# Modulation and gate vectors as TensorE strips instead of elementwise sums, with the recurrence's products regrouped

## The chip, the core and the metric

The kernel runs on one core of a Trainium2 chip. The metric is the device time of one execution in microseconds (us). Three executions of the kernel before took 2051.42, 2052.46 and 2072.93 us, median 2052.46. One further execution was profiled; all rows below come from it.

The engines are named as the profile names them: PE is TensorE, which multiplies, PEld is its loading of the stationary operand, DVE is VectorE, ACT is ScalarE, POOL is GpSimd, SP is SyncE, whose queue issues most transfers (DMAs). TensorE's results go to PSUM, in banks of 128 x 512 fp32.

## What is computed

A two-layer trunk over 256 latent and 256 context tokens of width 2048. A conditioning vector is turned into a shift, a scale and a gate for each layer, once for latent (`sc`) and once for context tokens (`scc`):

```python
sc = jax.nn.silu(c)
scc = jax.nn.silu(c_ctx)
for l in range(DEPTH):                       # 2 layers
    shift_l, scale_l, gate_l = split(sc @ mod_w[l] + mod_b[l])     # mod_w[l]: 2048 x 6144
    shift_c, scale_c, gate_c = split(scc @ mod_w[l] + mod_b[l])
    hl = xl * (1.0 + scale_l) + shift_l
    hc = xc * (1.0 + scale_c) + shift_c
    # layer 0: one input projection -> [pooling mixer | bidirectional RWKV-7] -> gate -> output projection
    # layer 1: one input projection -> attention -> gate -> output projection
    xl = layer_norm(ALPHA * xl + gate_l * yl, ln_g[l], ln_b[l])
    if not last: xc = layer_norm(ALPHA * xc + gate_c * yc, ln_g[l], ln_b[l])
```

The RWKV recurrence (16 heads, both directions) is computed in 8 chunks of 64 tokens: inside a chunk by Gram matrices and a triangular inverse, from chunk to chunk through a 64 x 64 state per head.

## The kernel before

Large weights come as fp32, are split into two fp32r halves (`whi` by ACT, `wlo` by POOL or DVE, lines 192 and 74), and every product is made of three fp32r matmuls (`mm3`): rows `acc<-hh,whi`, `acc<-hl,whi`, `acc<-hh,wlo`, each 128 x 128 by 128 x 512. These are the filling. The small products of the recurrence are fp32; the trace shows each fp32 product as two rows, and it names operands moving one first or last, so `cz<-AR,S` and `cx<-S,AR` are both products of a state `S` with `AR`.

What stands where on TensorE is written by a planner: TensorE's order is the order of recording (`manual_schedule`), the other engines are ordered by a scheduler. Each process is a Python generator that records some products and yields a number of microseconds; `merge` runs the process of the highest priority that is ready by an estimated time `self.t`, to which `mm` (line 86 issues every product) adds a cost. `share` scales that cost. The processes are

- `rwkv`, with one pass of 8 heads-pairs `p`: `prep(p+1)` and its `gram`s run while `chain(p)` runs; then `by_token`, `inverse`, `join`;
- `chain`: 8 steps `c`. A step makes `cx` = state times `AR`, adds `NV` on DVE to get `R`, then `cz` = `X` times `R`, copied to `U` by DVE and ACT, then `cs` = `BKT` times `U` for the next state, then the output `cy`: for each of four quadrants (2 directions x 2 heads) a product `GR` x `U` over all 128 rows and a product `S` x `AR` over 64 rows, in turn;
- `gram`: per direction, groups of four products of 64 rows x 128 columns, one head after the other, into the two banks `tr`;
- `fill0`: the input projection of layer 0 (to about 1290 us), then the output projection (`out0`) and layer 1;
- `gemvs0` and `gemvs1`: gates and layer 1's modulation. For each of 32 pieces of 256 columns, 8 loads of 256 KB (`gw`); DVE multiplies by the latent vector and adds (line 782); for the context vector ACT multiplies in place (line 778) and POOL adds (line 785). At a piece's end `gemv_end` sums over the partitions on TensorE (with `ones`, or four transposes and a DVE reduction). 24 pieces run beside the recurrence, the last 8 (only the latent vector, DVE alone) beside layer 1's projections;
- layer 0's modulation (`mod_units`, `mod_cols`) is already made on TensorE in the first 150 us: the vectors stand as 32 columns (`sc`), four 32-column strips of the array take four row blocks of the weights side by side, and a product with `comb` folds the strips.

`prep` and `tr` are PSUM tags of two banks, `cx` and `cz` of one each.

Of the kernel before, what the change touches and what calls it, by code (L numbers as in the profile page):

```python
# [14 lines left out]
KT = D // 128  # L15
# [21 lines left out]
class Kern:  # L37
# [50 lines left out]
    def tp(self, out, x, ident):  # L88
        self.t += 0.058
        self.nc.tensor.transpose(out, x, ident)  # L90
# [41 lines left out]
    def setup(self):  # L132
        nc, io, cp = self.nc, self.io, self.cp
        self.par = cp.tile([128, NPAR], F32, name="par")
        nc.sync.dma_start(self.par, io["par"])
        self.cv = cv = cp.tile([128, 32], F32, name="cv")
        nc.scalar.activation(cv, self.par[:, COL["cvec"]:COL["cvec"] + 32], AF.Silu)
        self.modc = [cp.tile([128, KT, 2, 2], F32, name=f"modc{i}") for i in range(2)]

    def setup2(self):  # L140
# [15 lines left out]
        self.ones = cp.tile([128, 1], F32, name="ones")  # L156
        nc.vector.memset(self.ones, 1.0)
# [39 lines left out]
    def mod_units(self, w, n, tag, done):  # L197


        nc = self.nc  # L200
        ps = []

        def f(q):
            def g(t):
                if q == 0:
                    ps.append(self.pt(tag, (128, n)))
                for j in range(4):
                    self.mm(ps[0][32 * j:32 * j + 32, :], self.sc[:, 4 * q + j, :], t[:, j * n:(j + 1) * n], start=(q == 0), stop=(q == KT // 4 - 1), share=0.25)
                yield 0.0
                if q == KT // 4 - 1:  # L210
# [5 lines left out]
        return [(w[:, q * 4 * n:(q + 1) * 4 * n], f(q), True) for q in range(KT // 4)]  # L216

    def mod_cols(self, layer, which, k0, n, tag, then=None):

        def done(row):  # L220
            yield 2.0
            nk = n // 128
            pc = self.pt("prep", (128, nk, 2))
            for j in range(nk):
                self.mm(pc[:, j, :], row[:, j * 128:(j + 1) * 128], self.comb)
            b = COL["modb"] + layer * 48 + which * KT + k0
            self.nc.vector.scalar_tensor_tensor(out=self.modc[layer][:, k0:k0 + nk, which, :], in0=pc, scalar=float(which),
                                                in1=self.par[:, b:b + nk].unsqueeze(2).to_broadcast([128, nk, 2]), op0=ALU.add, op1=ALU.add)
            if then:
                yield from then()  # L230
        return self.mod_units(self.io["modA"][which * 8 + k0 // 2], n, tag, done)
# [4 lines left out]
    def begin(self):  # L236
# [5 lines left out]
        with self.tc.tile_pool(name="beg", bufs=3) as bp:  # L242
            wp = self.wp
            self.wset(bp, 1024, 8, 6)

            self.sc = bp.tile([128, KT, 32], F32, name="sc", bufs=1)
            nc.gpsimd.memset(self.sc, 0.0)
# [1140 lines left out]
```

## Time and profile before

| | us |
|---|---|
| median of three executions | 2052.46 |
| the profiled execution | 2059.26 |
| its span, first to last instruction | 2057.4 |
| PE busy | 1845.3 (90%) |
| DVE busy | 1397.4 (68%) |
| POOL busy | 984.7 (48%) |
| ACT busy | 891.0 (43%) |
| mean granted TensorE clock | 0.942 of 2.4 GHz |

From 0 to 150 us the first modulation and projections run, from 150 to about 1250 the recurrence with the input projection as filling, to about 1500 layer 0's output projection, to 1660 the keys and values of layer 1, then attention and the last projection. In a timeline row the first number is the start, the second the length; rows of one line that follow each other are merged (xcount). Products are pipelined, so a row's length is longer than its distance to the next row, and the distance is what a product costs.

### The profile page before, as it was taken

Reading aid. Unit: us, or ns where it says so; the run is one execution under the profiler, and the core shown is the slowest. Engines: PE = TensorE matmul, PEld = TensorE weight load, DVE = VectorE, ACT = ScalarE, POOL = GpSimd, SP = SyncE. Lnnn points to the kernel's source line nnn. Section 1 sums busy time; section 2 is a strip of 40 time slices with the busy share of each in tenths; the row PEclk is TensorE's granted clock in tenths of the full one; section 3 lists DMA queues with packets and bytes.
Section 4 is the critical chain, followed back from the end, with each engine's and each line's share of the span. In section 5 each row is a group of like instructions: output and inputs, shape, how many; then the busy total and the mean of one; then the engine's idle time right before and its main releaser. Section 6 shows DMA issues by size and latency. Waiting matters only on the chain. (4 is left out here: it accounts for less than half of the span.)

```text
span 2057.4 us, 36816 instructions
## 1 busy us (share of the span) xinstructions
PE 1845.3 (90%) x13632; PEld 1351.9 (66%) x13632; DVE 1397.4 (68%) x2520; ACT 891.0 (43%) x1794; POOL 984.7 (48%) x931
## 2 busy tenths in 40 slices
PE   6887998998989999899898999889987999999895
PEld 3664566666666666666666677567755677888774
DVE  1234477777887877877878865646689467668457
ACT  1126545344453453544545533322244255555434
POOL 1114466656666665565665634644548242222224
PEclk9997989999998999999999999999999999999997
DMA  9866544334343343332433324576664553433654
GB/s 350 318 240 235 189 133 135 116 95 140 98 139 116 111 143 100 120 127 94 141 101 113 129 68 129 185 229 201 206 210 134 181 172 124 133 128 120 217 183 167
DMA packets 194804, 322.57 MB, mean 157 GB/s; under 512 B 17560, under 2 KB 93760, under 8 KB 193472
## 3 DMA queue, kind: packets, MB, share of 16 engines
q1 hardware_dynamic: 186272, 299.13, 43.6%
q10 hardware_dynamic: 8352, 21.09, 3.1%
q8 instruction: 107, 1.75, 0.4%
q14 instruction: 73, 0.60, 0.1%
HBM read 290.24 MB, written 29.91 MB: 156 GB/s over the span
## 5 line engine op out<-in xcount | busy, mean ns | idle before, releaser
L74 POOL TENSOR_TENSOR wlo<-wrow,whi 128x512 fp32r<-128x512 f32 (+1 forms) x348 | 489.0, 1407 | 643.9 <-ACT whi L192 575.1
L192 ACT CAST whi<-wrow 128x512 fp32r<-128x512 f32 (+1 forms) x528 | 327.3, 624 | 446.6 <-PE acc L86 111.3
L782 DVE SCALAR_TENSOR_TENSOR ga<-gw,cv,ga 128x256 f32<-128x256 f32 x480 | 350.1, 729 | 102.3 <-DMA gw<-in_modB 96.7
L86 PE MATMUL acc<-hh,wlo 128*128 128x512 f32 (+1 forms) x992 | 393.7, 397 | 8.9 <-POOL wlo L74 5.2
L86 PE MATMUL acc<-hh,whi 128*128 128x512 f32 (+1 forms) x992 | 390.1, 393 | 12.4 <-ACT whi L192 10.2
L86 PE MATMUL acc<-hl,whi 128*128 128x512 f32 (+1 forms) x992 | 391.8, 395 | 0.0
L785 POOL TENSOR_TENSOR ga<-gw,ga 128x256 f32<-128x256 f32 x336 | 290.8, 865 | 184.2 <-ACT gw L778 122.8
L778 ACT ACTIVATE gw<-gw,cv 128x256 f32<-128x256 f32 x384 | 190.8, 506 | 227.3 <-DVE ga L782 169.3
L86 PEld LDWEIGHTS acc<-hh,wlo 128*128 128x128 f32 x992 | 195.2, 197 | 54.4 <-issue 10.7
L86 PEld LDWEIGHTS acc<-hh,whi 128*128 128x128 f32 x992 | 194.5, 196 | 54.2 <-ACT whi L192 14.2
L86 PEld LDWEIGHTS acc<-hl,whi 128*128 128x128 f32 x992 | 194.6, 196 | 43.7 <-issue 12.7
L74 DVE TENSOR_TENSOR wlo<-wrow,whi 128x512 fp32r<-128x512 f32 (+1 forms) x180 | 140.9, 789 | 118.7 <-ACT whi L192 118.1
L86 PE MATMUL tr<-wlo,hh 128*128 128x512 f32 x224 | 91.9, 410 | 5.5 <-DVE wlo L74 3.0
L86 PE MATMUL tr<-whi,hh 128*128 128x512 f32 x224 | 90.8, 406 | 0.0
L86 PE MATMUL tr<-whi,hl 128*128 128x512 f32 x224 | 90.6, 404 | 0.0
L86 PE MATMUL tr<-AR,BK 64*128 64x128 f32 x512 | 83.9, 304 | 4.6 <-DVE GR L477 4.6
L86 PEld LDWEIGHTS tr<-AR,BK 64*128 64x128 f32 x512 | 68.3, 202 | 29.5 <-issue 21.6
L86 PE MATMUL cz<-GR,U 128*64 128x64 f32 x512 | 77.7, 245 | 8.0 <-ACT U L620 8.0
L86 PE MATMUL cz<-AR,S 64*64 64x64 f32 x448 | 75.4, 250 | 0.0
L86 PEld LDWEIGHTS cz<-GR,U 128*64 128x64 f32 x512 | 48.0, 140 | 23.1 <-ACT U L620 10.9
L641 ACT COPY AR<-cz 128x64 f32<-128x64 f32 x128 | 21.0, 215 | 94.0 <-PE cz L86 93.2
L86 PE MATMUL acc<-wlo,hh 128*128 128x512 f32 x128 | 52.2, 408 | 6.1 <-DVE wlo L74 5.7
(355 smaller groups left out, 3392.8 us busy)
## 6 DMA issues: line engine op xcount, KB each, us to landing
gw<-in_modB SPq DMA_DIRECT2D x256, 256.0 KB
wrow<-in_wA SPq DMA_DIRECT2D x176, 256.0 KB
wrow<-in_modA SPq DMA_DIRECT2D x64, 512.0 KB
wrow<-in_w SPq DMA_DIRECT2D x112, 256.0 KB
wrow<-in_woA SPq DMA_DIRECT2D x80, 256.0 KB
wrow<-in_wo SPq DMA_DIRECT2D x80, 256.0 KB
wrow<-in_w1g SPq DMA_DIRECT2D x64, 256.0 KB
pd<-ev SPq DMA_DIRECT2D x50, 256.0 KB
```

The costliest lines, as they stand in the source:

```text
L74: e.tensor_tensor(out=out, in0=raw, in1=hi.bitcast(F32), op=ALU.subtract)
L86: self.nc.tensor.matmul(out, a, b, start=start, stop=stop)
L192: self.lastsplit = self.nc.scalar.copy(hi, raw)
L641: nc.scalar.copy(AR[d][:, 1, c, :], cy[:, d, :])
L778: nc.scalar.activation(w[:, j, :], w[:, j, :], AF.Identity, scale=c)
L782: nc.vector.scalar_tensor_tensor(out=acc[:, v - vs[0], :], in0=w[:, j, :], scalar=c, in1=acc[:, v - vs[0], :], op0=ALU.mult, op1=ALU.add)
L785: nc.gpsimd.tensor_tensor(out=acc[:, 1, :], in0=w[:, j, :], in1=w[:, 0, :] if q == 0 else acc[:, 1, :], op=ALU.add)
```

## The change

1. `gemvs` replaces `gemv`, `gemv_end`, `gemvs0` and `gemvs1`: 64 pieces of 128 columns, each in four rounds `q`. A round loads 256 KB and makes four strip products (32 columns of `sc`, moving 128 columns of the weights) into a quarter of one `prep` bank, which is held for all 256 rounds. Rounds are recorded in threes, with 6.5 us of planner time behind each three. After a piece's fourth round DVE copies the quarter (128 x 128) to `grow`; behind the three, `columns` makes one product with `comb` into the other `prep` bank and DVE adds the bias. All 64 pieces run beside the recurrence. The gates leave as columns, by four stores of 2048 single elements.
2. `chain`: the four `S` x `AR` products of `cy` move from between the `GR` products to right behind the four of `cx`; `cx`, `cy` share one bank and `cz`, `cs` the other, exchanged at each step.
3. `gram` and the transposes in `by_token` alternate the two heads, into two banks, and their DVE or ACT copies follow both.
4. `lora`: the 64-row correction products become 128-row products with zeros in the other half.
5. `share=0.5` on the recurrence's small products: the planner counts half their cost. In `prep` the wait for `lora` moves ahead of the first `prep` product.

```diff
-        self.modc = [cp.tile([128, KT, 2, 2], F32, name=f"modc{i}") for i in range(2)]
+        self.modc = [cp.tile([128, KT, 3, 2], F32, name=f"modc{i}") for i in range(2)]
...
+    def strips(self, ps, w, n, q, last):
+        for j in range(4):
+            self.mm(ps[32 * j:32 * j + 32, :], self.sc[:, 4 * q + j, :], w[:, j * n:(j + 1) * n], start=(q == 0), stop=last, share=0.25)
+
+    def columns(self, layer, which, k0, row):
+        nk = row.shape[-1] // 128
+        pc = self.pt("prep", (128, nk, 2))
+        for j in range(nk):
+            self.mm(pc[:, j, :], row[:, j * 128:(j + 1) * 128], self.comb)
...
-        xl = self.rt([128, 2, 512], "BKT0", F32R)
+        xl = [self.rt([128, 2, 512], "BKT0", F32R), self.rt([128, 2, 512], "BK", F32R, bufs=2)]
+        for j in range(2):
+            nc.gpsimd.memset(xl[j][rows[1 - j]].bitcast(F32), 0.0)
...
-                    self.mm(pw, W[2 * j + d][rows[j], ps], xl[rows[j], d, :], start=False)
+                    self.mm(pw, W[2 * j + d][:, ps], xl[j][:, d, :], start=False)
...
         for cc in range(0, 8, 4):
-            for h in range(2):
-                hs = slice(64 * h, 64 * h + 64)
-                g = self.pt("tr", (128, 4, 128))
-                for c in range(cc, cc + 4):
-                    self.mm(g[:, c - cc, :], BK[hs, c, :, :], AR[hs, :, c, :])
-                    if c % 2:
-                        yield 0.0
+            g = [self.pt("tr", (128, 4, 128)) for _ in range(2)]
+            for c in range(cc, cc + 4):
+                for h in range(2):
+                    hs = slice(64 * h, 64 * h + 64)
+                    self.mm(g[h][:, c - cc, :], BK[hs, c, :, :], AR[hs, :, c, :], share=0.5)
...
         for d in range(2):
+            pq = [self.pt("tr", (128, 8, 64)) for _ in range(2)]
+            for c in range(8):
+                for h in range(2):
+                    hs = slice(64 * h, 64 * h + 64)
+                    self.tp(pq[h][:, c, :], st["BK"][d][hs, c, :, :], cst["ident"][hs, hs], share=0.5)
...
                 for d, h, hs in quads:
-                    self.mm(cx[hs, d, :], AR[d][hs, 0, c, :], S[hs, d, :])
+                    self.mm(cx[hs, d, :], AR[d][hs, 0, c, :], S[hs, d, :], share=0.5)
+                for d, h, hs in quads:
+                    self.mm(cy[hs, d, :], S[hs, d, :], AR[d][hs, 1, c, :], start=(d == 0), stop=False, share=0.5)
...
             for d, h, hs in quads:
-                self.mm(cy[hs, d, :], U[h][:, d, c, :], GR[h][:, d * 8 + c, :], stop=(c == 0))
-                if c:
-                    self.mm(cy[hs, d, :], S[hs, d, :], AR[d][hs, 1, c, :], start=False)
+                self.mm(cy[hs, d, :], U[h][:, d, c, :], GR[h][:, d * 8 + c, :], start=(c == 0 and d == 0), stop=(d == 1), share=0.5)
...
+    def gemvs(self):
+        nc, pool = self.nc, self.rp
+        def loads():
+            for i in range(64):
+                src = self.io["modB"][i // 4].rearrange("p (k c) -> p k c", k=KT)
+                for q in range(4):
+                    w = pool.tile([128, 4, 128], F32, tag="gw", name="gw", bufs=3)
+                    nc.sync.dma_start(w, src[:, 4 * q:4 * q + 4, i % 4 * 128:i % 4 * 128 + 128])
+                    yield w.rearrange("p k c -> p (k c)")
...
+        bank, row = self.pt("prep"), None
+        for r in range(256):
+            i, q = divmod(r, 4)
+            pg = bank[:, i % 4 * 128:i % 4 * 128 + 128]
+            self.strips(pg, ws.pop(0), 128, q, q == 3)
+            ahead()
+            if q == 3:
+                row = pool.tile([128, 128], F32, tag="grow", name="grow")
+                nc.vector.tensor_copy(row, pg)
+            if r % 3 == 2 or r == 255:
+                yield self.GPACE
+                if row is not None:
+                    j = (r - 3) // 4 if q < 3 else i
+                    layer, which = (0, 2) if j < 16 else (1, j // 16 - 1)
+                    self.columns(layer, which, j % 16, row)
+                    row = None
+                    if which == 2 and j % 16 == 15:
+                        for v in range(2):
+                            nc.sync.dma_start(self.gated[layer, v].rearrange("(k p) -> p k", p=128), self.modc[layer][:, :, 2, v])
+
+    GPACE = 6.5
```

The order of TensorE's instructions at two places. First, one step of `chain` from its third product on, before: `cs` (`U` by `BKT`), then `cy`, `GR` and `AR` in turn. A row is one product, or `xN` equal ones.

```order
L86 MATMUL cx<-U_2154,BKT_2156 64x64
L86 MATMUL cx<-U_2155,BKT_2157 64x64
L86 MATMUL cx<-U_2154,BKT_2156 64x64
L86 MATMUL cx<-U_2155,BKT_2157 64x64
L86 MATMUL cz<-GR_1249,U_2154 64x64
L86 MATMUL cz<-AR_1245,S 64x64
L86 MATMUL cz<-GR_1250,U_2155 64x64
L86 MATMUL cz<-AR_1245,S 64x64
L86 MATMUL cz<-GR_1249,U_2154 64x64
L86 MATMUL cz<-AR_1246,S 64x64
L86 MATMUL cz<-GR_1250,U_2155 64x64
L86 MATMUL cz<-AR_1246,S 64x64
```

The same step of the change on the same engine, its first products (with a `prep` product of `prep(p+1)` and a three of strip rounds behind them):

```order
L86 MATMUL cz<-S,AR_1244 64x64 x2
L86 MATMUL cz<-S,AR_1245 64x64 x2
L86 MATMUL cz<-AR_1244,S 64x64 x2
L86 MATMUL cz<-AR_1245,S 64x64 x2
L86 MATMUL prep<-T,cc 128x512
L86 MATMUL prep<-comb,grow 128x2
L86 MATMUL prep<-gw,sc 32x128 x12
```

and its third product on:

```order
L86 MATMUL cx<-U_2173,BKT_2175 64x64
L86 MATMUL cx<-U_2174,BKT_2176 64x64
L86 MATMUL cx<-U_2173,BKT_2175 64x64
L86 MATMUL cx<-U_2174,BKT_2176 64x64
L86 MATMUL cz<-GR_1248,U_2173 64x64
L86 MATMUL cz<-GR_1249,U_2174 64x64
L86 MATMUL cz<-GR_1248,U_2173 64x64
L86 MATMUL cz<-GR_1249,U_2174 64x64
```

The four `AR` products no longer stand between the `GR` products; they follow the step's first four, which have the same shape. Where a step has a three of rounds, twelve strip products stand between its first and its second product.

Second, such a three on TensorE with what each product waits for (DMAHW: a load; DVE: VectorE), here the rounds 3, 4 and 5:

```order
L86 MATMUL prep<-gw,sc 32x128 [waits DMAHW3_49]
L86 MATMUL prep<-gw,sc 32x128 x3
L86 MATMUL prep<-gw,sc 32x128 [waits DMAHW4_49,DVE_49]
L86 MATMUL prep<-gw,sc 32x128 x3
L86 MATMUL prep<-gw,sc 32x128 [waits DMAHW6_49]
L86 MATMUL prep<-gw,sc 32x128 x3
```

Round 3 ends a piece; round 4 writes the same bank and waits for DVE's copy of it. Of the 256 rounds 42 have such a wait inside a three; before, no product stood in this place.

## Rows read from the trace of the kernel before

**Rows 1.** Windows of the recurrence and of layer 1's start (us; busy, count).

```profile
core 0: us, PE busy (x) PEld busy (x) DVE busy (x) ACT busy (x) POOL busy (x), PEclk, DMA share, GB/s
300.00:1250.00 950.00, 872.77 (x8824) 630.54 (x8823) 744.73 (x1359) 452.82 (x956) 561.38 (x579) 0.95 0.36 115
1500.00:1660.00 160.00, 132.45 (x548) 98.32 (x548) 113.74 (x217) 60.81 (x127) 76.48 (x64) 0.95 0.53 177
```

**Rows 2.** Groups of instructions, 300 to 1250: the removed DVE work.

```profile
L782 DVE SCALAR_TENSOR_TENSOR ga<-gw,cv,ga 128x256 f32<-128x256 f32 x323 | 234.5, 726 | 48.8 <-DMA gw<-in_modB 46.2
```

**Rows 3.** What PE waited for, 300 to 1250: total us, times, longest.

```profile
PE cx L86 <- DVE U L619: 17.4, 15, 2.2
```

**Rows 4.** The same from 1500 to 1660.

```profile
PE prep L90 <- DVE hraw L950: 14.3, 6, 4.2
```

**Rows 5.** Timeline of PE: cs and cy of a step, full clock.

```profile
755.52 0.45 PE L86 MATMUL cx<-U,BKT 128*64 128x64 f32 x8
755.80 0.28 PE L86 MATMUL cz<-GR,U 128*64 128x64 f32 x2
...
757.81 0.50 PE L86 MATMUL acc<-hh,whi 128*128 128x512 f32 x1
```

**Rows 6.** Timeline of PE: cs and cy of a first step, without S.

```profile
1255.12 0.51 PE L86 MATMUL cx<-U,BKT 128*64 128x64 f32 x7
...
1255.85 0.50 PE L86 MATMUL acc<-hh,wlo 128*128 128x512 f32 x1
```

**Rows 7.** Timeline of PE: a small group between fill products.

```profile
660.63 0.39 PE L86 MATMUL acc<-hh,whi 128*128 128x512 f32 x1
660.95 0.45 PE L86 MATMUL cz<-R,X 64*64 64x64 f32 x8
661.33 0.51 PE L86 MATMUL acc<-hl,whi 128*128 128x512 f32 x1
661.67 0.40 PE L86 MATMUL acc<-hh,wlo 128*128 128x512 f32 x1
661.90 0.39 PE L86 MATMUL acc<-hh,whi 128*128 128x512 f32 x1
```

**Rows 8.** Timeline of PE: Gram group, transposes, and alternating 64-row products.

```profile
655.94 1.16 PE L86 MATMUL tr<-AR,BK 64*128 64x128 f32 x8
657.02 1.12 PE L86 MATMUL prep<-T,cc 128*128 128x512 f32 x2
...
700.55 2.08 PE L86 MATMUL tr<-cc,vsh 64*64 64x64 f32 x64
...
707.40 0.71 PE L90 MATMUL tr<-cc,BK 64*128 64x64 f32 x8
```

**Rows 9.** Timeline of PE: layer 0's strips and a comb group.

```profile
84.09 3.79 PE L86 MATMUL prep<-wrow,sc 128*32 128x256 f32 x64
...
94.72 0.50 PE L86 MATMUL prep<-comb,wrow 128*128 128x2 f32 x4
```

**Rows 10.** Timeline: TensorE waits for a DVE result.

```profile
619.14 0.28 DVE L613 TENSOR_TENSOR R<-cx,NV 128x128 f32<-128x128 f32 x1
...
619.57 0.45 PE L86 MATMUL cz<-R,X 64*64 64x64 f32 x8 [0.41 <-DVE R L613]
```

**Rows 11.** Timeline of PE: the removed ends of gemv.

```profile
242.47 1.02 PE L86 MATMUL prep<-ga,ones 128*1 128x256 f32 x4
...
630.80 0.66 PE L90 MATMUL prep<-cc,ga 128*128 128x128 f32 x4
```

**Rows 12.** Timeline: a prep bank written, and ACT reading it.

```profile
748.44 1.02 PE L86 MATMUL prep<-T,cc 128*128 128x512 f32 x2
...
750.52 0.67 ACT L430 ACTIVATE M<-prep,e 128x512 f32<-128x512 f32 x1
```

**Rows 13.** Windows: the granted clock behind idle gaps.

```profile
634.00:640.00 6.00, 5.03 (x27) 2.75 (x28) 4.09 (x10) 3.43 (x8) 4.47 (x5) 0.75 0.71 218
640.00:654.00 14.00, 14.00 (x62) 10.22 (x62) 6.20 (x15) 2.67 (x6) 3.51 (x5) 0.50 0.30 96
```

More of the change, by code (lines that the diff above doesn't have):

```diff
@@ L194, in split, with mod_cols, done @@
         return hi, lo
-    def mod_units(self, w, n, tag, done):
+    def strips(self, ps, w, n, q, last):
[6 more added lines that the diff above has]
+            self.mm(pc[:, j, :], row[:, j * 128:(j + 1) * 128], self.comb)
+        b = COL["modb"] + layer * 48 + which * KT + k0
+        self.nc.vector.scalar_tensor_tensor(out=self.modc[layer][:, k0:k0 + nk, which, :], in0=pc, scalar=float(which == 1),
+                                            in1=self.par[:, b:b + nk].unsqueeze(2).to_broadcast([128, nk, 2]), op0=ALU.add, op1=ALU.add)
+    def mod_cols(self, which, k0, n, tag, then=None):
         nc = self.nc
         ps = []
+        def done(row):
+            yield 2.0
+            self.columns(0, which, k0, row)
+            if then:
+                yield from then()
         def f(q):
@@ L214, in f @@
             return g
[L216 to L231, printed above, removed]
+        w = self.io["modA"][which * 8 + k0 // 2]
+        return [(w[:, q * 4 * n:(q + 1) * 4 * n], f(q), True) for q in range(4)]
     FIRST = (M_WD, M_AD, M_R, M_K, M_V, M_R + 1)
@@ L420, in prep @@
             yield 8.0
+            if lora:
+                yield lora
             pk = self.pt("prep")
@@ L817, in gemvs0 @@
-    def gemvs0(self):
-        yield 0.0
-        for i in range(24):
-            yield from self.gemv(i, self.rp, self.GPACE, True)
-        for p in self.gemv_ends:
-            yield p
-    GPACE = 3.6
-    def gemvs1(self):
-        for i in range(24, 32):
-            yield from self.gemv(i, self.ln, 3.0, False)
-        for p in self.gemv_ends:
-            yield p
+    def gemvs(self):
[7 more added lines that the diff above has]
+                    yield w.rearrange("p k c -> p (k c)")
+        loads, ws = loads(), []
+        ahead = lambda: ws.extend(w for w in [next(loads, None)] if w is not None)
+        for _ in range(3):
+            ahead()
+        yield 10.0
+        bank, row = self.pt("prep"), None
[3 more added lines that the diff above has]
+            self.strips(pg, ws.pop(0), 128, q, q == 3)
+            ahead()
+            if q == 3:
+                row = pool.tile([128, 128], F32, tag="grow", name="grow")
[10 more added lines that the diff above has]
+                            nc.sync.dma_start(self.gated[layer, v].rearrange("(k p) -> p k", p=128), self.modc[layer][:, :, 2, v])
@@ L1299, in run @@
         self.rates = 0
-        self.gemv_ends, self.gtag = [], "prep"
         self.bns = {}
```

108 lines of the change are left out of this document (22 added, 86 removed).

## Prediction

> **What bounds the kernel now.** I read the table of busy times first: PE is busy for 90% of the span and no other engine above 68%, so a gain must come from PE's own rows or from its idle time. The windows place the idle time: in the stretch in which this change works, 300 to 1250, PE is busy 872.77 of 950 us and so idle for 77, at a granted clock of 0.95 of 2.4 GHz; from 1500 to 1660 it is idle 27.5 [rows 1]. The list of waits says for whom: for `U` of the chain (DVE) 17.4 us in 15 waits [rows 3], and behind it many entries of 1 to 6 us, nearly all results of DVE or ACT. In layer 1 the longest is `hraw`, 14.3 us in 6 waits [rows 4], which DVE makes between the sums of `gemvs1`. DVE's largest work in the recurrence is just those sums, 234.5 us [rows 2]. So two things can pay: fewer PE rows, and a DVE that answers sooner. The price is new PE rows.
>
> The sum is made against the profiled execution, 2059.3 us (span 2057.4), which is 6.8 above the median of the three. PE durations are read at full clock and divided by 0.95, the clock of the stretch [rows 1].
>
> **Regrouped chain: -77.** `cs` and `cy` of a step take from 755.52 to 757.81, 2.29 us [rows 5]. In a first step, which has no state, the same `cs` and the four `GR` products take 0.73 [rows 6]. The four `S` x `AR` products, in turn with products of another height, thus cost 1.56. Put behind four of their own shape they cost what equal small products cost: eight rows between fill products raise the distances to .32, .38, .34 and .23 where the fill alone has .23 [rows 7], that is .58 extra; the length .45 less about .22 that any row outlasts its distance, over 7, is .033 a row. So the eight rows cost .26, and the rest, .31, is the price of entering and leaving a small shape. Saved: 1.56 - .26 = 1.30 a step, in 8 x 7 steps with a state: 56 x 1.30 / .95 = 77. The bounds are 60 (the group's ends are not hidden any more) and 87 (nothing is left).
>
> **Gram and transposes: -33 and -8.** A `gram` group of four 64-row products takes 1.08 [rows 8]; 64 groups / .95 = 73. If two heads in the two row halves ran wholly side by side, half would go (-36); if not at all, nothing. Rows that alternate halves stand in the trace: `vsh`, 64 rows in 2.08 or .032 each [rows 8], against .033 for the 64-column rows above, which also alternate quadrants; neither shows a lone half. Since `cy` shows that the order of shapes is worth more than a factor of two, I take -33, near the upper bound. The 32 groups of transposes, .71 each [rows 8], are 24 us; half would be 12, and I take -8.
>
> The Trainium skill's page "TensorE: Matmul & The Clock Gate" (Part 3, "Measured speedup vs the span model") gives four row tiles a speedup of 3.07, not 4. By an estimate from it two tiles are worth about 1.55; gram then gives -26, and the whole sum is 7 us more. No row here shows two tiles side by side.
>
> **Full-height corrections in `lora`: -10.** 32 half-height products no longer pay the .31 of a change of shape: 32 x .31 / .95.
>
> **Ends of `gemv` removed: -24.** 8 with two products by `ones` at 1.02 [rows 11], 8 with one at half that, and 16 with four transposes; these are 128 x 128 and cost about what eight 64-row ones do, .71 [rows 8]: (8.2 + 4.1 + 11.4) / .95.
>
> **Strips: +87.** Layer 0's strips take 3.79 for 64 rows of 256 columns [rows 9]; less the .3 that a row outlasts its distance, 54 ns each. Here a row has 128 columns. Bounds: 27 ns (half the columns) and 54 (no gain from the smaller number). The small rows above also cost about 33 ns for 64 columns, which would make 27 optimistic, but strips go side by side in four column groups, and I take 27. A three has 24 rows and one entering: .65 + .31 = .96; 86 threes / .95 = 87. The upper bound is 146.
>
> **`columns`: +17.** Two `comb` products take .50 [rows 9], so one .25; it stands among strips and small rows: 64 x .25 / .95.
>
> **Copies inside threes: +42.** DVE's copy of a finished quarter reads the bank that the next round writes, and the order shows PE waiting for it in 42 rounds with nothing between to hide it. Behind such a product the strip products and, as PE is in order, the chain's next product and all filling are queued. The nearest row: a DVE operation of .28 ends at 619.42 and the waiting product begins .15 later [rows 10]; with the time until the last strip's result is there I take 1.0 each. The lower bound is .6 (25 us), the upper the longest wait for `U`, 2.2 [rows 3], 92 us.
>
> The Trainium skill's page "PSUM — Partial Sum Buffer" ("PSUM bank collisions raise a hardware error") says that engines must be kept apart by bank and quadrant, not by address. The wait on DVE in the order agrees with it. If the address decided, the waits would be needless and the sum 42 us less.
>
> **One `prep` bank instead of two: +13.** The strips hold the other for all of the recurrence. A bank written from 748.44 is read by ACT until 751.19 [rows 12], so a `prep` product that follows another within two microseconds now waits. I counted 13 such places in the order of after, a `comb` product often one of the two, at 1.0 each; 0 if filling always stands between, 30 if all pay the 2.2 of `U`.
>
> **Smaller loads and stores: +5.** Four stores of 2048 single elements and loads whose runs are 512 bytes instead of 1 KB have no row. Only layer 0's output waits for the first stores, some hundred us later: 0, and 15 if SP's queue holds the weights' loads behind them.
>
> **Relief: -36 and -20.** With the 234.5 us gone [rows 2] (64 copies and 64 small sums come in), DVE falls from 78% to near 55% of the stretch [rows 1], and ACT and POOL lose their share. Idle on results of DVE and ACT is most of the 77. `U`, `R` and `S` already have priority, so a wait shrinks only by what stood ahead on DVE at that moment, up to .73 of one sum; I take not quite half, 36 (bounds 10 and 60). What is late next is the chain itself: product, copy, product. In layer 1 `gemvs1` goes as a whole: the 14.3 of `hraw` and some of the low halves that DVE makes, 20 of 27.5 idle (bounds 10 and 25).
>
> **Sum.** -77 - 33 - 8 - 10 - 24 + 87 + 17 + 42 + 13 + 5 - 36 - 20 = -44: 2015 against 2059.3, and 2008 against the median. PE's own work nets about nothing; the gain is the relief.
>
> **Rivals.**
> - *A, slower: PE stops in the middle of threes.* Each of the 42 waits costs the upper bound of 2.2, and the clock pays too: where PE stood idle for .97 of 6 us the granted clock averaged .75, and for the next 14 us, without a gap, it was .50, half speed, the 1.2 GHz level [rows 13]. Fourteen us at half speed lose 7; if one gap in five does that, a gap costs 3.6, 42 of them 151 in place of 42: 2117. The point: above 2.05 us a gap there is no gain. For it speak the regular place of the gaps; against it that 1.0 is made of short rows. Chance .16.
> - *B, larger gain.* The copies are mostly hidden, as PE's rows outlast their distance (14 in place of 42), and the relief in the recurrence is 55 instead of 36: 2008 - 28 - 19 = 1961. For it speaks that DVE's backlog is the change's main target; against it that waits are short. Chance .20.
> - *C, no difference.* Pairs of half-height products do not overlap (+41), or the strips cost 54 ns (+59), as the 33 ns of 64-column rows hints: 2049 to 2067. Chance .22.
> - My forecast, 1985 to 2032, has .42.
>
> **How the numbers follow.** About 1% is what a measurement of this kernel can tell from no change: under 2032 is faster, over 2073 slower. Faster is my forecast and B, .62; same is C, .22; slower is A, .16. The range takes in B to 1950 and C to 2068; outside stay A and a little of B. The forecast's own range is 1985 to 2032.
>
> **What would show it.** In the chain the rows `cs` and `cy` together take .7 to .8 instead of 2.29, with no half-height row between; else the regrouping failed. A `gram` group of both heads (16 rows) takes about 1.1; at 2.2 there is no overlap. 24 strip rows take about .65, and where a piece ends inside a three a gap stands before the next strip with DVE's `grow` copy as its cause, about 1.0 in 42 places; near 0 is B, over 2 with a granted clock under .90 in the stretch is A. `hraw` is gone from the waits; DVE is near 55%. What would make me wrong most easily is the strips' price and the planner: it now counts half for small products and puts 64 pieces where 24 stood, so the chain's steps may stand closer to their results than before and wait for them in spite of a free DVE.

## The result, and the profile after

The changed kernel takes 1964.99 us in the median of four executions (1958.94 to 1968.86); the kernel before, in four executions beside them, 2062.69. The ratio is 0.9524, 95% interval 0.9448 to 0.960: faster by 4.8%. Forecast were 2008 us with a range of 1950 to 2068. The direction and the range held, but the gain is more than twice the forecast's, and it came in another way than the forecast said.

The profiled execution took 1968.86 us, its span is 1967.1, so 90 us less than before. PE is busy for 1751.2 us of it (89%), DVE for 1018.4 (52%, before 68%), ACT for 723.3 and POOL for 666.9. The stretch of [rows 1], and PE's waits from 150 to 1250 us, in the changed kernel (columns as in [rows 1] and [rows 3]):

```profile
300.00:1250.00 950.00, 850.35 (x10699) 613.14 (x10684) 497.74 (x1082) 317.35 (x648) 311.44 (x285) 0.95 0.49 139
```

```profile
PE prep L86 <- DVE grow L795: 45.9, 42, 5.9
PE prep L86 <- DMA gw<-in_modB: 12.4, 3, 9.7
```

DVE fell from 745 to 498 us, and the waits for `U` have left the top of the list. In their place stand the 42 waits inside the threes that the order of instructions had shown: 45.9 us in 42 times, 1.09 each. `hraw`, in layer 1, is down from 14.3 us [rows 4]:

```profile
PE prep L90 <- DVE hraw L925: 4.5, 5, 2.6
```

The timeline of PE shows the new rows (start, length; the distance to the next row is the cost):

```profile
604.67 0.28 PE L86 MATMUL prep<-comb,grow 128*128 128x2 f32 x2
604.88 0.86 PE L86 MATMUL prep<-gw,sc 128*32 128x128 f32 x24
605.67 1.13 PE L86 MATMUL prep<-rsh,cc 128*128 128x512 f32 x2
...
612.66 1.16 PE L86 MATMUL tr<-AR,BK 64*128 64x128 f32 x16
613.75 0.45 PE L86 MATMUL cx<-U,BKT 128*64 128x64 f32 x8
614.03 0.40 PE L86 MATMUL cz<-GR,U 128*64 128x64 f32 x8
614.37 0.38 PE L86 MATMUL prep<-comb,grow 128*128 128x2 f32 x2
```

24 strip rows cost .79; sixteen `gram` rows, both heads, 1.09 where two groups took 2.16 [rows 8]; `cs` and the four `GR` products .62, where they and the four `AR` products in turn took 2.29 [rows 5]. The `AR` products now stand behind `cx`:

```profile
640.52 0.45 PE L86 MATMUL cx<-S,AR 64*64 64x64 f32 x8
640.80 0.40 PE L86 MATMUL cx<-AR,S 64*64 64x64 f32 x8
641.13 0.50 PE L86 MATMUL acc<-hh,whi 128*128 128x512 f32 x1
```

If each row of PE's timeline is given its distance to the next, without the idle time, and the rows are added by kind over the whole span, the two traces differ so (us):

| | before | after | difference | forecast |
|---|---|---|---|---|
| the chain's products | 191.4 | 103.7 | -88 | -77 |
| `gram` | 78.4 | 35.3 | -43 | -33 |
| transposes of `BK` | 20.5 | 12.5 | -8 | -8 |
| `lora` (64 products) | 33.1 | 19.8 | -13 | -10 |
| ends of `gemv` | 20.1 | 0 | -20 | -24 |
| strips | 0 | 79.7 | +80 | +87 |
| `comb` of the pieces | 0 | 16.8 | +17 | +17 |
| filling and projections (5087 rows both times) | 1246.8 | 1231.6 | -15 | 0 |
| PE idle at strips (copies 45.9, loads 12.4) | 0 | 58.2 | +58 | +47 |
| PE idle elsewhere | 191.1 | 136.0 | -55 | -43 |

(The last forecast is the relief of 56 less the 13 of the single `prep` bank.) So most terms were about right, and the misses, most of them on the same side, add up to 46 us with the rows not listed. The 15 us of the filling are the clock: if each of these rows is weighed with the clock granted during it, the sums are 1186 us of full clock before and 1188 after. All of PE's rows together fall from 1847 to 1752 us, while its idle time goes from 191 to 194 us. But a table of differences does not say which part earned what; for that there are experiments.

### The profile page after: what moved, and what is told of

Read it like the earlier page. It is cut to its first block, busy times and chain, and to the rows that moved or that the text cites. A ratio compares the mean times of both kernels' runs of the same rounds, so it can differ in the third digit from the quotient of the medians.

```text
span 1967.1 us, 39217 instructions
## 1 busy us (share of the span) xinstructions
PE 1751.2 (89%) x15696; PEld 1305.2 (66%) x15696; DVE 1018.4 (52%) x2079; ACT 723.3 (37%) x1410; POOL 666.9 (34%) x573
## 5 line engine op out<-in xcount | busy, mean ns | idle before, releaser
L74 POOL TENSOR_TENSOR wlo<-wrow,whi 128x512 fp32r<-128x512 f32 (+1 forms) x348 | 469.6, 1351 | 1044.7 <-ACT whi L195 888.6
L86 PE MATMUL prep<-gw,sc 128*32 128x128 f32 x2048 | 85.7, 285 | 58.3 <-DVE grow L795 45.9
L86 PEld LDWEIGHTS prep<-gw,sc 128*32 128x32 f32 x2048 | 48.9, 111 | 78.1 <-DVE grow L795 57.4
L213 DVE SCALAR_TENSOR_TENSOR modc<-prep,par 128x2 f32<-128x2 f32 (+1 forms) x80 | 12.3, 154 | 85.3 <-PE prep L86 85.1
L86 PEld LDWEIGHTS tr<-wlo,hh 128*128 128x128 f32 x224 | 42.9, 192 | 19.9 <-DVE wlo L74 7.2
L86 PE MATMUL acc<-whi,hh 128*128 128x512 f32 x128 | 53.9, 421 | 2.3 <-ACT hh L78 2.3
L447 POOL TENSOR_TENSOR BK<-T,D 64x512 f32<-64x512 f32 x32 | 47.0, 1470 | 25.4 <-DVE T L442 17.3
L86 PE MATMUL prep<-wrow,sc 128*32 128x256 f32 x512 | 39.4, 444 | 17.1 <-DMA wrow<-in_modA 16.9
L86 PE MATMUL acc<-whi,hl 128*128 128x512 f32 x128 | 53.0, 414 | 0.3 <-POOL hl L74 0.3
L483 DVE TENSOR_TENSOR GN<-tr,cc 128x256 f32<-128x256 f32 x64 | 26.8, 419 | 45.2 <-PE tr L86 45.2
```

The costliest lines, as they stand in the source:

```text
L74: e.tensor_tensor(out=out, in0=raw, in1=hi.bitcast(F32), op=ALU.subtract)
L86: self.nc.tensor.matmul(out, a, b, start=start, stop=stop)
L447: nc.gpsimd.tensor_tensor(out=BK[hs, :, 1 - h, :], in0=c8(k)[hs], in1=c8(ew)[hs], op=ALU.mult)
L483: nc.vector.tensor_tensor(out=GN[h][:, u, :], in0=g[h][:, :, 0:64], in1=cst["gmask"][:, 0:1, :].to_broadcast([128, 4, 64]), op=ALU.mult)
```

## The experiments

The other comparisons ran beside executions of the kernel before of their own, so ratios are compared, not times.

**Each half alone.** The first keeps the strips and puts back the recurrence's products, with the planner's full count of them, as before; the second does the reverse, with the half count of the change.

```diff
# strips only: the changed kernel, with chain, gram, by_token and lora of before
-                for d, h, hs in quads:
-                    self.mm(cy[hs, d, :], S[hs, d, :], AR[d][hs, 1, c, :], start=(d == 0), stop=False, share=0.5)
...
# regrouping only: the kernel before, with chain, gram, by_token and lora of the change
+                for d, h, hs in quads:
+                    self.mm(cy[hs, d, :], S[hs, d, :], AR[d][hs, 1, c, :], start=(d == 0), stop=False, share=0.5)
...
```

> The changed gates and modulation alone (strips, columns, the stores as columns); the recurrence's products stand as before. In the traces the changed kernel has 94 us less PE work than before and the same idle time (194 against 191). Theory 1 (the two halves add): the regrouped chain, gram, transposes and lora are worth 88 + 43 + 8 + 13 = 152 us of PE work, so the other half costs about 62: this run is 3% slower than before (ratio 1.02 to 1.04), with about 76 us more PE work (80 strips, 17 comb, 20 of the old ends gone), 46 us of waits for the copy of a piece, and about 60 us less of other idle time. Theory 2 (the halves need each other: the freed elementwise engines only pay once the products stand together): the idle time does not fall here and the ratio is above 1.05. Theory 3 (strips pay by themselves, as the forecast's sum of -43 for relief and strips hoped): 0.99 to 1.01.

> The regrouping alone (chain, gram, transposes, lora, half cost for the planner); gates and modulation on the three elementwise engines as before. Theory 1 (the halves add): 152 us of PE work go and nothing comes, ratio 0.92 to 0.935, better than the changed kernel. Theory 2 (the elementwise engines become the bound of the recurrence): DVE has 745 us of work in the 950 us of the stretch, the stretch shrinks by some 120 us, DVE goes to about 90%, and PE's idle time on DVE and ACT grows by 40 to 100 us: ratio 0.945 to 0.97, no better than the changed kernel.

Strips only: 1.0171 (1.0105 to 1.0237), one to two per cent slower. Regrouping only: 0.9896 (0.9856 to 0.9937). Alone the two would add to +0.7%; together they give -4.8%. The regrouping takes 128 us of PE work out here too (1847 to 1719 us), but PE's idle time grows from 191 to 300. Its waits from 150 to 1250 us, and its end of the recurrence:

```profile
PE cx L86 <- DVE S L638: 32.0, 14, 4.2
PE tr L90 <- DVE U L499: 31.8, 15, 3.6
PE cz L86 <- DVE S L638: 21.7, 9, 3.4
PE cx L86 <- DVE R L620: 14.4, 7, 4.2
```

```profile
1180.00:1300.00 120.00, 76.38 (x1014) 54.86 (x1014) 65.43 (x134) 27.96 (x64) 35.12 (x44) 0.70 0.26 80
```

DVE's results for the chain are late, and from 1148 us on nothing is left to fill the waits with: 95 us of the recurrence run with no filling at a clock of 0.65, and behind a short piece of filling another 50 us, from 1275. In these two stretches lie 67 us of the idle time; from 150 to 1100 us it is 143 against 84 before. Both parts of that rise speak against theory 1 of the regrouping. Theory 2 has the direction, but not the size: the ratio is above its 0.945 to 0.97, and DVE did not go to 90%, it is busy 653 us of the 850 from 300 to 1150 (77%, before 79%). With the strips alone the parts are near theory 1 of that expectation (72 us more work, 1847 to 1919, where it had 76; 49 us of waits at the strips; other idle time 92 us less, where it had 60), and the ratio lies just below its 1.02 to 1.04. Theories 2 and 3 fall. What fails is that the two halves add.

**The waits inside threes.** Rounds in twos end a group at each piece's end:

```diff
-            if r % 3 == 2 or r == 255:
+            if q % 2:
                 yield self.GPACE
-                if row is not None:
-                    j = (r - 3) // 4 if q < 3 else i
+                if q == 3:
+                    j = i
...
-    GPACE = 6.5
+    GPACE = 4.35
```

> The changed kernel with rounds recorded in twos (4.35 us of planner time behind each) instead of threes, so that a piece always ends a group and no round waits for DVE's copy with nothing between. Theory 1 (the 42 waits of together 46 us are a loss on the path, as the forecast's term of 42 says): they vanish, 42 more groups pay .31 each, 13 us; net -33, ratio to before about 0.936 (0.93 to 0.942). Theory 2 (what stood waiting for the copy waits for the next result of the chain instead, and TensorE's filling is late anyway): the waits on U, R and S grow by about as much, ratio 0.95 to 0.956.

0.9333 (0.9291 to 0.9374): theory 1. PE's idle time at the strips falls from 58 to 20 us, nearly all of it for loads, and the waits on the chain's results do not grow in its place (idle elsewhere 136 to 143). So the copies stood on the path. Of the 42 waits 18 took .41, as in [rows 10]: there DVE took the copy at once. In the other 24 the copy stood in DVE's queue behind other work, and they bring the mean to 1.09; the median is .63. The longest, DVE's timeline:

```profile
825.19 1.23 DVE L432 TENSOR_TENSOR_SCAN D<-cc,D 128x512 f32<-128x512 f32 x1 [6.02 <-DMA D<-sgd]
...
828.52 0.73 DVE L336 SCALAR_TENSOR_TENSOR T<-raw,par,T 128x512 f32<-128x512 f32 x1
829.18 0.27 DVE L795 COPY grow<-prep 128x128 f32<-128x128 f32 x1
```

and PE's:

```profile
823.17 0.43 PE L86 MATMUL prep<-gw,sc 128*32 128x128 f32 x8
829.50 1.08 PE L86 MATMUL prep<-gw,sc 128*32 128x128 f32 x16 [5.91 <-DVE grow L795]
```

DVE itself stood 6.02 us in front of an instruction whose load was late (`D<-sgd`), with the copy queued behind it, and PE stood behind the copy. Nothing of the kind is seen in front of the next longest (3.99 and 2.38 us): there DVE had worked for 18.6 and 5.9 us without a break before it came to the copy.

**The planner's count.** The changed kernel with every `share=0.5` set to 1:

```diff
-                    self.mm(cx[hs, d, :], AR[d][hs, 0, c, :], S[hs, d, :], share=0.5)
+                    self.mm(cx[hs, d, :], AR[d][hs, 0, c, :], S[hs, d, :], share=1.0)
...
```

> The changed kernel with the planner counting the recurrence's small products in full again (share 1 in place of 0.5); the products themselves are unchanged. Theory 1 (the half cost places filling and does little else): PE work within 5 us of the changed kernel, ratio 0.947 to 0.957. Theory 2 (with the full cost the planner lets fewer fill products pass between two chain products, so they stand closer to their results): PE's waits on U, R, S and the tr results grow by 15 to 40 us, ratio 0.96 to 0.972.

0.9348 (0.9305 to 0.939): faster than the change, which neither theory had. What the half count did shows at the end of the recurrence. The changed kernel, then this one:

```profile
1180.00:1300.00 120.00, 91.02 (x899) 60.37 (x899) 55.68 (x86) 35.54 (x74) 52.49 (x53) 0.79 0.47 140
```

```profile
1180.00:1300.00 120.00, 98.77 (x527) 68.65 (x526) 55.14 (x88) 38.34 (x76) 66.55 (x54) 0.94 0.61 186
```

With half the count more filling is placed beside each step of the chain (from 300 to 1100 us 37 rows a step, with the full count 33). It is used up at 1230 us, and the last 50 us of the recurrence run bare, with 21 us of idle time and at a clock of 0.69. With the full count the longest stretch without filling at the end of the recurrence is 14 us. The mean clock is 0.965 instead of 0.951. Counted in full, strips alone stand at 1.0171, the regrouping alone at 0.9894 (below), and both at 0.9348.

**Both, and the regrouping again with its filling.**

> The changed kernel with both: rounds in twos, and the small products counted in full. Theory 1 (two separate losses: 42 waits inside threes, and a bare end of the recurrence, 1230 to 1281 us in the changed kernel): the gains add, ratio about 0.916 (0.910 to 0.923). Theory 2 (both only take up the same slack, and the recurrence's own latency sets its end): no better than either alone, 0.93.

Rounds in twos and the full count together: 0.9265 (0.9214 to 0.9317), the fastest of these kernels, 1906.69 us in the median. The gains add in part: next to the full count alone the median falls by 22 us, idle time by 37 while the 42 more groups and their neighbours add 11 of work, next to twos alone by 19. So theory 1's 0.916 was too good and theory 2's 0.93 is just inside the interval. The clock of the stretch is 0.98:

```profile
300.00:1250.00 950.00, 882.31 (x10992) 631.17 (x10991) 545.13 (x1123) 332.84 (x684) 334.53 (x307) 0.98 0.51 148
```

> The regrouping alone again, as in the run with only the regrouping, but with the planner counting the small products in full. There the filling ended at 1148 us and 95 us of the recurrence ran bare, at a clock of 0.76; so its idle time (300 us against 191 before) has two candidate causes. Theory 1 (DVE, ACT and POOL bound it: idle between 150 and 1100 us also rose, from 84 to 144 us): even with filling to the end it stays well above the kernel with strips at full cost (ratio 0.935): 0.96 to 0.975. Theory 2 (only the bare tail): it falls to what the missing PE work is worth, 0.93 to 0.94.

The regrouping alone with the full count: 0.9894 (0.9846 to 0.9942), no better than with the half count. PE's idle time is 294 us: from 300 to 1250 PE is busy 784 us of 950 and the clock is 0.92.

```profile
300.00:1250.00 950.00, 784.13 (x8756) 575.29 (x8756) 740.66 (x1333) 456.61 (x962) 565.15 (x588) 0.92 0.39 121
```

But the edit did not do what the expectation asks, filling to the end. Two stretches of 42 and 49 us still run bare (with the half count 95 and 50):

```profile
1195.00:1237.00 42.00, 20.38 (x558) 15.94 (x558) 20.25 (x36) 14.19 (x27) 11.85 (x14) 0.69 0.37 114
1268.00:1317.00 49.00, 29.93 (x233) 16.75 (x233) 28.17 (x45) 11.07 (x30) 19.22 (x21) 0.69 0.43 132
```

They hold 41 us of the idle time. (The clock of 0.76 in the expectation is that of 1100 to 1300 us; in the 95 bare us it was 0.65.) From 150 to 1100 us, where filling was there, it is 160 us against 84 before, which is theory 1's side, and three quarters of the rise. So theory 2, only the bare end, falls, but the bare end remains a part of the cause, and what the regrouping alone would be worth with filling to the end is not shown. In the kernels with strips and the full count no such stretch is left: there the strips, too, are work that covers the chain's waits. As measured, without the move of the gates to TensorE, the regrouping is worth 1%.

**DVE's sums, taken away.** The same edit in the regrouping alone and in the kernel before:

```diff
                     elif q + j == 0:
                         nc.vector.tensor_scalar(acc[:, v - vs[0], :], w[:, j, :], c, None, op0=ALU.mult)
-                    else:
+                    elif not helped:
                         nc.vector.scalar_tensor_tensor(out=acc[:, v - vs[0], :], in0=w[:, j, :], scalar=c, in1=acc[:, v - vs[0], :], op0=ALU.mult, op1=ALU.add)
```

> The kernel before with the same DVE sums left out (only the time counts): the relief by itself, without strips and without the regrouping. Theory 1 (the forecast's relief term: 36 us in the recurrence, half of its idle time): ratio 0.975 to 0.985, idle time 191 to about 155. Theory 2 (with the products ungrouped there is enough filling between the chain's steps to hide most of DVE's lateness): ratio above 0.99. The strips alone lowered the idle time from 191 to 148 us in spite of 49 us of waits of their own, which speaks for more than theory 1: 0.965 or less would be that.

> The regrouping alone at full cost, and DVE's sums for the gates and layer 1's modulation left out beside the recurrence (each piece keeps its first product only, so those vectors are wrong and the run shows time alone); loads, ACT's products and POOL's sums stay. With the sums the ratio was 0.989 and TensorE's idle time 294 us. Theory 1 (DVE's backlog delays the results that the regrouped chain waits for): idle falls to 150 to 210 us and the ratio to 0.93 to 0.955. Theory 2 (ACT's and POOL's share of the sums, or the chain's own length, bounds it): idle stays above 250, ratio 0.975 or more.

In the kernel before: 0.973 (0.9686 to 0.9773), 56 us. That is the relief by DVE's sums, with the waits for loads in front of them [rows 2], and it is larger than the 36 us of the forecast's term, just beyond theory 1's range, which its interval touches. In the trace idle time falls by 32 us (191 to 159), about as forecast; the mean clock of this execution is 0.962 instead of 0.942, and the same filling takes 19 us less:

```profile
300.00:1250.00 950.00, 898.99 (x9108) 649.70 (x9108) 590.52 (x1077) 462.58 (x992) 564.24 (x603) 0.98 0.40 125
```

So what comes beyond the idle time is the clock: at full clock the filling is 1188 us here and 1186 before. (The profiled execution is the fastest of its kernel, 1991 us; the other three had clocks of 0.951 to 0.957, the kernel before in the executions beside them 0.934 to 0.946.)

In the regrouping alone, with the full count: 0.9675 (0.9633 to 0.9716), 45 to 50 us less than with the sums, between the two theories; and 269 us of idle time stay, which is theory 2's side. Of these, 41 lie in two bare stretches at the end, as with the sums. Of the 141 us from 150 to 1100, 80 end with a result of DVE's and 52 with one of ACT's, though DVE is now busy for 482 us of the 800 from 300 to 1100, with the sums 641. One thing that stands in front of such results is a load. ACT's waits from 300 to 1100 us in this kernel, and DVE's in the regrouping with the sums and the full count:

```profile
ACT gw L780 <- DMA gw<-in_modB: 174.4, 98, 5.1
```

```profile
DVE ga L784 <- DMA gw<-in_modB: 64.5, 42, 6.5
```

What stands behind such a wait in an engine's queue comes late too. In the timeline of the regrouping without sums:

```profile
355.01 1.31 ACT L780 ACTIVATE gw<-gw,cv 128x256 f32<-128x256 f32 x3 [4.01 <-DMA gw<-in_modB]
...
355.64 0.83 DVE L782 TENSOR_SCALAR ga<-gw,cv 128x256 f32<-128x256 f32 x1 [3.79 <-DMA gw<-in_modB]
...
358.60 0.26 ACT L626 COPY U<-cx 64x128 f32<-64x128 f32 x1
...
358.92 0.69 PE L86 MATMUL cx<-U,BKT 128*64 128x64 f32 x8 [3.18 <-ACT U L626]
```

ACT idles 4.01 us for a load of the gates, works off what has piled up behind it, copies `U` late, and PE waits 3.18 us for `U`. In the changed kernel ACT waits for such loads only 4.1 us in the same stretch. DVE's waits were to be seen before: the idle column of [rows 2] has 46.2 us of waiting for `gw` in front of DVE's sums. But such waits do not decide by themselves. The kernel before without sums has them at ACT as well, with 159 us of PE idle time in all:

```profile
ACT gw L778 <- DMA gw<-in_modB: 115.5, 82, 4.6
```

How the rest of the idle time of the regrouping (some 75 us over the changed kernel's) is shared between these load waits, ACT's and POOL's own work on the gates, the bare end, and the strips' own time as cover between two products of the chain, is open: no run took these away one by one.

**What the `cy` regrouping saves.** In the kernel before, the eight products of `cy` in two other orders at the same place:

```diff
# grouped
             for d, h, hs in quads:
-                self.mm(cy[hs, d, :], U[h][:, d, c, :], GR[h][:, d * 8 + c, :], stop=(c == 0))
-                if c:
-                    self.mm(cy[hs, d, :], S[hs, d, :], AR[d][hs, 1, c, :], start=False)
+                self.mm(cy[hs, d, :], U[h][:, d, c, :], GR[h][:, d * 8 + c, :], start=(d == 0), stop=(c == 0 and d == 1))
+            if c:
+                for d, h, hs in quads:
+                    self.mm(cy[hs, d, :], S[hs, d, :], AR[d][hs, 1, c, :], start=False, stop=(d == 1))
# staggered (gr and ar issue one GR and one AR product; their definitions and the lines taken out are left out here)
+                gr(0, 0, True, False)
+                ar(0, 1, True, False)
+                gr(1, 0, False, False)
+                ar(1, 1, False, False)
+                gr(0, 1, False, False)
+                ar(0, 0, False, False)
+                gr(1, 1, False, True)
+                ar(1, 0, False, True)
```

> The kernel before with one edit: in cy the four GR products stand first and the four S x AR products behind them, at the same place of the step; nothing else moves. Theory 1 (the price is the change between products of 128 and of 64 rows, eight times a step): cs and cy take 2.29 us before and 1.1 to 1.4 here; 56 steps make about 55 us of PE work less. Theory 2 (moving them behind cx is what pays): 2.2 us or more stays. Theory 3 (the price is that each S x AR product adds to the PSUM columns that the product right before it wrote): as theory 1, 1.1 to 1.4, since here four products lie between.

> The kernel before with the eight products of cy still in turn, GR then AR, but each S x AR product adds to columns that another product wrote three to five places earlier, not the one right before. Theory 1 (changing the height costs): as before, cs and cy 2.1 to 2.4 us a step. Theory 3 (adding to columns just written costs): 1.0 to 1.4 us.

One step of PE's timeline, grouped:

```profile
760.63 0.45 PE L86 MATMUL cx<-U,BKT 128*64 128x64 f32 x8
760.92 0.40 PE L86 MATMUL cz<-GR,U 128*64 128x64 f32 x8
761.25 0.45 PE L86 MATMUL cz<-AR,S 64*64 64x64 f32 x8
761.63 1.16 PE L86 MATMUL tr<-AR,BK 64*128 64x128 f32 x8
```

and staggered:

```profile
763.21 0.45 PE L86 MATMUL cx<-U,BKT 128*64 128x64 f32 x8
763.49 0.28 PE L86 MATMUL cz<-GR,U 128*64 128x64 f32 x2
763.70 0.32 PE L86 MATMUL cz<-AR,S 64*64 64x64 f32 x2
763.96 0.33 PE L86 MATMUL cz<-GR,U 128*64 128x64 f32 x2
...
765.50 1.12 PE L86 MATMUL prep<-rsh,cc 128*128 128x512 f32 x2
```

Grouped, the step takes 1.00 us; staggered 2.29, to the hundredth what it took before. All `GR` and `AR` rows of `cy` together are 46.8 us grouped, 118.8 staggered and 121.0 before. Which columns are added to does not matter, so theory 3 falls, and the order of shapes is what costs: theory 1. The staggered step has six changes of shape more than the grouped one and takes 1.29 us more, about .2 a change. Part of that may be that two half-height products that follow each other overlap and two apart do not; no run separates this. Nor is it the number of rows alone: the grouped step costs .99 in the median whether a product of 128 rows follows or, as here, `tr<-AR,BK` with 64 rows and 128 columns instead of 64, and in the changed kernel the last row of a group of strips (128 rows, 32 columns) costs .20 where a row inside it costs .025.

The move behind `cx` adds little: the four `AR` products cost .38 here and .33 behind `cx` in the changed kernel, where the `cx` in front of them no longer pays for leaving its shape (.28 instead of .38). The grouped kernel, one execution, took 2026.65 us where the kernel before took 2061.24 (the staggered one 2052.83): 76 us less PE work in the chain, but 27 us more idle time, and the filling 16 us longer at a clock of 0.936. A part of the price came back here as well.

**What `gram` saves.** The changed kernel, with both banks in turn but one head after the other:

```diff
-            for c in range(cc, cc + 4):
-                for h in range(2):
-                    hs = slice(64 * h, 64 * h + 64)
-                    self.mm(g[h][:, c - cc, :], BK[hs, c, :, :], AR[hs, :, c, :], share=0.5)
+            for c in range(4):
+                for k in range(2):
+                    self.mm(g[k][:, c, :], BK[hs, c + 4 * k, :, :], AR[hs, :, c + 4 * k, :], share=0.5)
```

> The changed kernel with one edit: gram alternates two PSUM banks as in the change, but with products of one head (one half of the rows) in turn, and the other head behind. Theory 1 (two halves of the array work side by side when heads alternate): here nothing overlaps; 16 rows take 2.0 to 2.3 us instead of 1.10, and gram in all about 75 us instead of 35. Theory 2 (writing two banks in turn is what pays): 16 rows stay at about 1.1 us, 35 us in all.

```profile
616.31 2.05 PE L86 MATMUL tr<-AR,BK 64*128 64x128 f32 x16
618.29 0.50 PE L86 MATMUL acc<-hh,whi 128*128 128x512 f32 x1
```

Sixteen rows of one half take 1.98 us, those of two halves in turn 1.09; `gram` in all 63.3 against 35.3 us. Theory 1: the two halves of the array work side by side, and nearly wholly. The Trainium skill's page "TensorE: Matmul & The Clock Gate" (Part 3, "Measured speedup vs the span model") has 3.07 for four row tiles, from which the forecast estimated 1.55 for two; here it is 63.3 / 35.3 = 1.8, and the measurement decides. (63.3 and not 75 probably because two groups became one and so leave a small shape half as often.) This kernel took 1973.34 us in one execution, 0.960 of the kernel before beside it, where the changed kernel had 0.952: some 16 us for 28 us of PE work more. Its filling was 12 us shorter, at a clock of 0.962.

**The stores of single elements.** Twos and full count, with the four stores on ACT's queue:

```diff
-                            nc.sync.dma_start(self.gated[layer, v].rearrange("(k p) -> p k", p=128), self.modc[layer][:, :, 2, v])
+                            nc.scalar.dma_start(self.gated[layer, v].rearrange("(k p) -> p k", p=128), self.modc[layer][:, :, 2, v])
```

> Rounds in twos and full cost, and the four stores of 2048 single elements issued from ACT's queue instead of SP's. In all kernels with strips a strip waits for its load just behind the first two stores (9.7 us at 412 us in the changed kernel, 7 to 15 us in the others), because the loads stand behind the stores on SP's queue. Theory 1: that wait goes, 8 to 10 us less, ratio 0.922 to 0.9265 where 0.9265 was measured with SP's queue. Theory 2 (the wait has another cause, or the elements hold the engines that move data whichever queue they come from): the wait stays, ratio 0.9265.

0.9302 (0.9252 to 0.9352): nothing won. A strip still waits, at the same place as in the changed kernel at 412 us:

```profile
409.12 0.66 PE L86 MATMUL prep<-gw,sc 128*32 128x128 f32 x8 [10.82 <-DMA gw<-in_modB]
```

Theory 1 falls, and the trace shows the second form of theory 2. Transfers in two stretches of this kernel, in front of the stores (370 to 383 us) and behind them (388 to 401), with the time from issue to landing in the median:

```profile
gw<-in_modB SPq DMA_DIRECT2D x4, 256.0 KB, 3.9
wrow<-in_wA SPq DMA_DIRECT2D x2, 256.0 KB, 3.8
```

```profile
wrow<-in_wA SPq DMA_DIRECT2D x2, 256.0 KB, 16.1
gw<-in_modB SPq DMA_DIRECT2D x2, 256.0 KB, 17.6
```

The two stores are issued from ACT's queue at 384 us and land 17 and 20 us later; what SP's queue issues from 391 to 398 us lands from 408 to 411, soon after them. Away from the stores a `gw` load took 3.6 us in the median and 8.2 at most. Beside the second pair of stores, at 947 us, the weights' loads take 14 to 18 us, and with the stores on SP's queue it is the same (18.3 us for the load issued at 394 us in the changed kernel). So the loads are issued in time and their transfers last longer while the stores are under way; by what means is not shown.

## Why the prediction was right, and where its sum was not

- **The time** fell into the range, 1950 to 2068, but outside the forecast's own 1985 to 2032. It is close to rival B's time (1961) without B's reasons: the copies were not hidden at all, and PE's idle time in the recurrence, apart from the strips, fell by 36 us, the sum's 36 and not B's 55. The rest came from the chain, `gram` and the clock. That the range held is in part luck: its lower bound was set for B, whose copies and relief did not come.
- **Copies inside threes**: right in place, number and mean (42 gaps, 1.09 us against 1.0; six of the 42 passed rival A's 2.05). The way to 1.0 was not: a copy that DVE takes at once costs .41, and the mean is made by what stood in front of it in DVE's queue. That the two agree is luck.
- **Strips, `comb`, ends, transposes, `lora`**: within 7 us each. 27 ns a strip row was right (25 inside a group, 33 with leaving it, .79 for 24 rows); rival C's 54 ns fell.
- **Chain and `gram`**: right in mechanism and too small, by 11 and 10 us. The price of changing shapes was read rightly from [rows 5] and [rows 6], as the staggered order shows. 88 is a little beyond the stated bound of 87; by the forecast's own numbers the bound at which nothing is left is 1.56 x 56 / .95 = 92, and the `AR` products still cost 20 us. For `gram` two halves overlap almost fully.
- **Relief and the single `prep` bank**: the relief was right in size, 36 us in the recurrence and 18 behind it (forecast 20). The 13 us for the bank are not to be seen: all waits of other `prep` products from 150 to 1290 us are 9 us, before 19.
- **The clock** was left out, and it is the largest miss: the sum divides by 0.95 and stops there. The same filling ran 15 us faster, at a higher clock, though PE's idle time in all did not fall. Where the idle time lies seems to count (the bare stretches have 0.63 to 0.71), but what raised the clock of the changed kernel is not shown.
- **The reading of the sum failed**: that PE's own work nets about nothing and the gain is the relief. By its own terms the rows add up to -48 us and idle time to +4 (42, 13 and 5 of waits, less 56 of relief). Measured are 95 us less work and 3 us more idle time. Nor can the halves be priced one by one: alone the regrouping is worth 22 us (0.9894), though its rows are 152 us less in the changed kernel, and the strips cost 35 (1.0171). Alone most of what the regrouping saves turns into waits for DVE and ACT and into a bare end. With the strips it counts. DVE's sums are 45 to 50 us of the difference, as their removal alone shows; the rest is not divided between loads, the other engines' sums and the strips' own cover.
- **The relief's cause**: DVE's sums with the load waits in front of them are worth 56 us in the kernel before and 45 to 50 in the regrouping alone. What busy time and what load waits have in it was not separated.
- The note that the planner's half count might place the chain closer to its results was wrong in sign: it spent the filling early and left the end bare.

## What to carry to other kernels

Before work saved on the bound engine is counted as time, ask whom it then waits for: price the pair, and try each half alone. On an engine that also makes results for the critical chain, look not only at its busy time but at what stands in its queue in front of such a result, other work or a load that is late. In this kernel it paid to sort small products by their shape and to let products of the two row halves take turns; and filling should be spent so that it lasts to the end of the chain that it covers.

## What the runs showed of the hardware

A change between fp32 products of 128 rows and of 64 rows costs about .2 us: eight products in turn take 2.0 us, sorted .7; leaving strips of 32 columns for other products costs as much. Two row halves in turn give 1.8 times the rate of one half. Four 32-column strips in turn cost 25 ns a row of 128 columns inside a group, 33 with leaving it. Loads issued while a store of 2048 single elements was under way took up to 21 us to land instead of about 4, whichever queue the store came from. The mean granted clock went only roughly with the idle time: 0.923 with 300 us idle, 0.962 with 159 and 0.971 with 149, but with 186 to 194 us it was 0.942 (the kernel before), 0.951 (the change) and 0.965 (the change with the full count), and the strips alone had 0.942 with 148.
